# Prompt attention with value products in runs and 1024-column exponentials, reserved buffers, held first loads, and a last MLP step without Strassen's sums

## The chip, the cores and the metric

The kernel runs on one core of one Trainium2 chip. The core has TensorE for matmuls (PE in the profile, its weight loads PEld), VectorE (DVE), ScalarE (ACT), GpSimd (POOL) and SyncE (SP, which here only issues DMAs), an on-chip memory of 128 partitions (SBUF), and the matmul accumulators (PSUM, eight banks of 512 fp32 columns). The metric is device time in microseconds (us) of one execution, from the inputs in device memory to all outputs written. A lower time is better.

## What is computed

One inference step of a one-layer decoder: 2048 prompt tokens, and 8 sequences of 8 new tokens each with 8192 cached positions. Everything is fp32. Model width is 1024, the MLP's hidden width 4096.

- One input projection gives the queries, keys, values and forget gates of 8 attention heads of width 64 ("FoX"), and queries, keys, values and gates of 4 mLSTM heads of width 128.
- FoX attention of the prompt is causal softmax with a forgetting bias:

```python
s = jnp.einsum('bqhd,bkhd->bhqk', q_i, k).astype(jnp.float32) * scale
s = s + L_i[..., :, None] - L[:, :, None, :]
s = jnp.where(k_pos[None, :] <= q_pos[:, None], s, -jnp.inf)
p = jax.nn.softmax(s, axis=-1)
return jnp.einsum('bhqk,bkhd->bqhd', p.astype(v.dtype), v)
```

- The new tokens attend over their paged caches; the mLSTM heads run a chunked recurrence with a matrix state; the mLSTM output is normalised and multiplied by an output gate.
- Both are joined, go through the output projection, a residual layer norm, and the MLP:

```python
mix = jnp.concatenate([fox_h, mn.astype(x.dtype)], axis=-1) @ w_o
x1 = _layer_norm(DN_ALPHA * x + mix, ln1_g, ln1_b)
hid = jnp.square(jax.nn.relu(x1 @ w1))
return _layer_norm(DN_ALPHA * x1 + hid @ w2, ln2_g, ln2_b)
```

Outputs are the tokens, and keys, values, gates and states of prompt and samples.

## The kernel before

**Matmuls.** Large products are made of three fast matmuls: each operand is split into a rounded high part (`split_hi`, ACT, L154) and the rest (`split_lo`, DVE, L157); `mm3` (L162) multiplies high by high, high by low and low by high. Transposes and the value products of attention use plain fp32 matmuls.

**Order.** The program is written in Python and unrolled. A planner assigns each engine's instructions an order by a simulated time line; program order is the priority, so an instruction may be placed ahead of earlier ones when its operands and its buffer are ready in that simulation. On the chip each engine and each DMA queue keeps the planned order. `tc.issue_after(ins)` puts an instruction behind another of the same engine; `add_manual_dep` with class `Sync` makes it wait for another engine's instruction. Tiles come from pools; a tile name with `bufs=n` is a ring of n buffers. Pools of a later phase lie on the memory of pools that were closed, tiles in the order in which their names are first asked for, and the first write of a tile waits for the old tiles that lay there.

**Stages.**
1. Input projection (`block_a`, to about 888 us): four blocks of 512 prompt tokens. The mLSTM recurrence (`m_block`) and cached attention run between its pieces, a step at a time (`tick`, `beside`). Each mLSTM chunk ends in `norm_out` (L614): statistics on DVE, a power on POOL, four normalising instructions on DVE, the output gate's multiply on POOL (L627), then four transposes on PE (L632). In the last block's last value pass `begin_b` (L220) loads the first keys and queries of attention.
2. Prompt attention (`phase_b`, about 888 to 1338 us): 64 units, 8 heads × 8 groups of 256 queries. `scores` (L957) makes for each of two query tiles the products with the keys in pieces of up to 512 columns (L975, L976), adds the bias while taking the maximum on DVE (L982, L986) and puts the result into a score tile `S`. `values` (L993) takes the exponentials on ACT with their row sums (L1003), turns the probabilities on PE four 128×128 tiles at a time into a PSUM tile `pt` (L1016, three buffers), copies them to `PT` (ACT L1019 or DVE L1021), and multiplies by the values (L1025). Within a unit the products of four key tiles follow those four tiles' transposes. The scores of unit n+1 stand in the program ahead of the values of unit n. `head` takes the tiles of a head (values `vn`, bias `nl`, keys `ks`), in rings of two. POOL adds up parts of the second MLP weight in memory meanwhile (`w2_sum`).
3. Output projection and first layer norm (`phase_o`, to about 1562 us).
4. MLP (`phase_c`): four blocks of 512 prompt tokens; the last also holds the 64 sample rows. Each has 8 steps p. `hidden(p, half)` makes 256 hidden columns of either half; `output(p)` adds their product with `w2` to the result rows `y`. Output uses Strassen's scheme: a 2 × 2 split (token halves × hidden halves), seven products of sums instead of eight, sums of `w2` made ahead in memory, sums of hidden values on DVE (`made`, L1392), and each product added to one or more result parts (`add`, L1362). When a row's last contribution is in, `add` takes its statistics (L1370), and `norm_quick` (L187) normalises it and stores it.

Of the kernel before, what the change touches and what calls it, by code (L numbers as in the profile page):

```python
# [10 lines left out]
F32 = mybir.dt.float32  # L11
F32R = mybir.dt.float32r
# [13 lines left out]
S = 2048  # L26
# [26 lines left out]
def body(ctx, tc, I, O, stages):  # L53
# [166 lines left out]
    def begin_b():  # L220

        bf["kn"] = pf.tile([128, 512], F32, name="kn0")
        bf["qn"] = pf.tile([128, 256], F32, name="qn0")
        for d in range(2):
            SY.dma_start(bf["kn"][d * 64:d * 64 + 64], O["k_prompt"][0:64, 0:512])
        for d in range(2):
            SY.dma_start(bf["qn"][d * 64:d * 64 + 64], dq[0, 0:64, 0:256])

# [384 lines left out]

    def norm_out(hh, np_, og, tok0):  # L614

# [10 lines left out]
        hf = hh.rearrange("p h e -> p (h e)")  # L626
        G.tensor_tensor(hf, hf, og, op=OP.mult)  # L627

# [40 lines left out]
    def m_block(bi):  # L669
# [10 lines left out]
        for c in range(bi * 4, bi * 4 + 4):  # L680
# [41 lines left out]
            for p in range(2):  # L722
                yield 1
                pc = ppm.tile([128, 2, 129], F32, name="mn", tag="mm", bufs=2)
                for i in range(2):
                    T.matmul(pc[:, i], kw[:, 2 * p + i], va_[:, 2 * p + i], start=True, stop=True)
# [168 lines left out]
    def phase_b():  # L895
# [15 lines left out]
        def head(h):  # L911
            vn = Z[0]["vn"] if h == 0 else pb.tile([128, 16, 64], F32, name="vn", bufs=2)
            nl = pb.tile([128, 2048], F32, name="nl", bufs=2)
            if h == 0:
                masks.append(pb.tile([128, 128], F32, name="dmask"))
            ls = pb.tile([128, 32], F32, name="ls", bufs=2)
            ks = pb.tile([128, 2048], F32R, name="ks", bufs=2)
            G.memset(ls, 1.0)
            return dict(h=h, ls=ls, nl=nl, vn=vn, ks=ks)
# [7 lines left out]
        def keys_load(h, g):  # L927
            kn = pb.tile([128, 512], F32, name="kn", bufs=3)
            for d in range(2):
                SY.dma_start(kn[d * 64:d * 64 + 64], kp[h * 64:h * 64 + 64, g * 512:(g + 1) * 512])  # L930
            return kn
# [11 lines left out]
        def queries(z, g):  # L943

            h = z["h"]
            qn = bf["qn"] if h == g == 0 else pb.tile([128, 256], F32, name="qn", bufs=3)
# [3 lines left out]
            if h == 0 and g == 0:  # L950
                z["vn"] = pb.tile([128, 16, 64], F32, name="vn", bufs=2)
            ql = pb.tile([128, 256], F32R, name="ql", bufs=3)
            split_hi(qh, qn)
            split_lo(ql, qn, qh)
            z["q", g] = qh, ql

        def scores(z, g):  # L957
# [4 lines left out]
            for i in range(2):  # L962
# [8 lines left out]
                for a in range(0, n, 512):  # L971
# [21 lines left out]
        def values(z, g, sc):  # L993
# [3 lines left out]
            for i, (st, mx) in enumerate(sc):  # L997
                qt = 2 * g + i
                n = (qt + 1) * 128
                lp = pb.tile([128, 4], F32, name="lp", bufs=6)  # L1000
                for k, sp in enumerate(st):
                    w = min(512, n - k * 512)
                    last["ACT"] = A.activation(sp[:, :w], sp[:, :w], AF.Exp, bias=mx[:, 7:8], accum_out=lp[:, k:k + 1])  # L1003
                V.tensor_reduce(z["ls"][:, qt:qt + 1], lp[:, :len(st)], axis=AX.X, op=OP.add)

            po = ppb.tile([128, 256], F32, name="po", bufs=1)
            nk = 2 * g + 2
            for k0 in range(0, nk, 4):
                PT = pb.tile([128, 4, 256], F32, name="PT", bufs=4)
                for i in range(2):  # L1010
                    kk = min(4, 2 * g + i + 1 - k0)
# [3 lines left out]
                    for k in range(kk):  # L1015
                        T.transpose(pt[:, k], sc[i][0][k0 // 4][:, k * 128:(k + 1) * 128], ident)  # L1016
                    dst = PT[:, :kk, i * 128:i * 128 + 128]
                    if i == 0 or (k0 // 4) % 2 != 0:
                        A.copy(dst, pt[:, :kk])  # L1019
                    else:  # L1020
                        V.tensor_copy(dst, pt[:, :kk])  # L1021
                for k in range(k0, min(k0 + 4, nk)):
                    q0 = 128 if k == nk - 1 else 0
                    c = (k % 2) * 64
                    last["PE"] = T.matmul(po[c:c + 64, q0:], z["vn"][:, k], PT[:, k - k0, q0:],  # L1025
                                          start=(k < 2), stop=(k >= nk - 2), skip_group_check=True)
                tick(0.45 * min(4, nk - k0))
            if g % 4 == 0:
# [24 lines left out]

        masks = []
# [6 lines left out]
        dmask = masks[0]  # L1061
        pad(pb, 64)
# [6 lines left out]
        for n in range(len(units) + LA):  # L1069
            if 10 <= n < 16 and acc[1] is not None:  # L1070
                attend()
            w2_due[0] += 64 * (n % 8 // 2 + 1) / 130 if n >= 8 else 0
            while n and len(w2_done) < min(64, w2_due[0]):
                w2_sum()
# [201 lines left out]
    def phase_c():  # L1276
# [51 lines left out]
        for ci, blk in enumerate(CB):  # L1328
# [28 lines left out]
            def add(t, half, ps, op=OP.add):  # L1357
# [16 lines left out]
            def operands(p):  # L1374
# [39 lines left out]
            def output(p, ahead, begun=None):  # L1414
# [13 lines left out]
                for at_, n in enumerate(order):  # L1428
                    kind, first_, last_, r0, half, op = plan[n]
                    if p == 7 and at_ == 2 and ci == 3:  # L1430
                        C["gb"] = vecs(2)
                    for m in order[:at_ + 3]:
# [28 lines left out]
                if begun:  # L1461
                    for hf in range(2):
                        turn(ci + 1, 4, hf, begun)

            def y_out(t):
                return O["y_sample"].rearrange("b t d -> (b t) d") if t == 16 else O["y_prompt"][0, t * 128:(t + 1) * 128]
# [478 lines left out]
```

## Time and profile before

| | |
|---|---|
| Median of 3 runs | 3236.75 us (3231.51 to 3241.11) |
| Profiled execution | 3245.35 us |
| Its span, first to last instruction | 3242.4 us |
| PE, DVE, ACT, POOL busy | 96%, 65%, 46%, 28% |
| Mean granted TensorE clock | 0.987 |
| DMA | 734.34 MB, mean 226 GB/s |

Rows of the profile are read so: a line number (L1025) is that of the kernel; `out<-in` are tile names; `xN` counts instructions; in time lines the first number is the start in us, the second the duration, and a bracket at the end holds the idle time before it and what ended it. Busy time of PE includes the filling and draining of its pipeline, so neighbouring matmuls overlap in the list. Rows of line 154, 157, 163, 164, 165 belong to helpers and are told apart by their tiles.

### The profile page before, as it was taken

The numbers are of one execution on the slowest core, as the hardware profiler recorded it, in microseconds if no ns is written. First come the engines' busy times: TensorE is split into PE (matmuls) and PEld (weight loads), VectorE is DVE, ScalarE is ACT, GpSimd is POOL, SyncE is SP. The second block draws the span as 40 slices with busy tenths as digits, with TensorE's granted clock in tenths as the row PEclk, the third lists the DMA queues.
The fourth block names the chain that finished last, engine by engine and source line by source line (L and its number), as shares of the span: only waits on it lengthen the run. The fifth ranks groups of instructions, "written<-read, shape, count | busy, mean of one in ns | idle before, by whom it ended". The sixth has DMA issues, their size and how long they took to land. (4 is left out here: it accounts for less than half of the span.)

```text
span 3242.4 us, 57713 instructions
## 1 busy us (share of the span) xinstructions
PE 3127.7 (96%) x21585; PEld 2535.8 (78%) x21585; DVE 2095.6 (65%) x5062; ACT 1489.0 (46%) x2940; POOL 907.2 (28%) x974
## 2 busy tenths in 40 slices
PE   8899999999989999999999999999999999899997
PEld 8898998998956666677677777776777777698895
DVE  6866657456478788544466568656586665766658
ACT  3342343343378888522344345343454444344442
POOL 0021233323334333276233423433333121000000
PEclk9999999999989999999999999999999999999999
DMA  5465776866667776487887878868779766543322
GB/s 188 128 220 174 254 225 202 277 238 232 228 220 204 185 181 150 171 300 262 294 291 277 296 270 308 317 243 328 289 282 338 279 212 210 208 147 137 121 95 81
DMA packets 339775, 734.34 MB, mean 226 GB/s; under 512 B 63656, under 2 KB 177704, under 8 KB 338600
## 3 DMA queue, kind: packets, MB, share of 16 engines
q1 hardware_dynamic: 252360, 416.18, 39.2%
q0 software_dynamic: 83520, 304.12, 26.7%
q10 hardware_dynamic: 3616, 10.36, 0.9%
q8 instruction: 170, 2.79, 0.3%
q14 instruction: 109, 0.89, 0.1%
HBM read 677.71 MB, written 86.38 MB: 236 GB/s over the span
## 5 line engine op out<-in xcount | busy, mean ns | idle before, releaser
L157 DVE TENSOR_TENSOR wl<-wr,wh 128x1024 fp32r<-128x1024 f32 x300 | 366.0, 1222 | 249.5 <-ACT wh L154 241.9
L163 PE MATMUL ph<-x1h,wh 128*128 128x512 f32 (+1 forms) x1280 | 455.2, 356 | 0.0
L164 PE MATMUL ph<-x1l,wh 128*128 128x512 f32 (+1 forms) x1280 | 453.0, 354 | 0.2 <-DVE x1l L157 0.2
L165 PE MATMUL ph<-x1h,wl 128*128 128x512 f32 (+1 forms) x1280 | 450.5, 354 | 0.7 <-DVE wl L157 0.4
L154 ACT ACTIVATE wh<-wr 128x1024 fp32r<-128x1024 f32 x300 | 315.4, 1053 | 290.1 <-PE ph L164 162.4
L1662 POOL DMA_INDIRECT kT<-cache_k,idxK x256 | 275.8, 1077 | 540.7 <-PE sQ L1685 477.2
L163 PE MATMUL py<-wh,hh 128*128 128x512 f32 x896 | 358.3, 403 | 6.4 <-ACT hh L154 3.7
L164 PE MATMUL py<-wl,hh 128*128 128x512 f32 x896 | 352.4, 395 | 5.5 <-DVE wl L157 5.5
L165 PE MATMUL py<-wh,hl 128*128 128x512 f32 x896 | 349.2, 395 | 2.1 <-DVE hl L157 2.1
L1362 DVE TENSOR_TENSOR y<-y,py 128x512 f32<-128x512 f32 x416 | 281.5, 682 | 98.9 <-PE py L165 94.8
L163 PE MATMUL pm<-xh,whi 128*128 128x256 f32 (+1 forms) x1024 | 299.5, 292 | 0.0
L164 PE MATMUL pm<-xl,whi 128*128 128x256 f32 (+1 forms) x1024 | 295.5, 289 | 0.0
L165 PE MATMUL pm<-xh,wlo 128*128 128x256 f32 (+1 forms) x1024 | 294.5, 288 | 0.0
L1773 POOL DMA_INDIRECT vt<-cache_v,idxV x164 | 177.7, 1084 | 384.3 <-PE sO L1797 316.9
L163 PEld LDWEIGHTS ph<-x1h,wh 128*128 128x128 f32 x1280 | 241.2, 188 | 40.8 <-issue 7.8
L165 PEld LDWEIGHTS ph<-x1h,wl 128*128 128x128 f32 x1280 | 240.3, 188 | 37.1 <-issue 3.7
L164 PEld LDWEIGHTS ph<-x1l,wh 128*128 128x128 f32 x1280 | 241.2, 188 | 34.4 <-issue 3.3
L163 PE MATMUL pm<-whi,xh 128*128 128x256 f32 (+2 forms) x816 | 238.1, 292 | 9.4 <-ACT whi L154 8.4
L164 PE MATMUL pm<-wlo,xh 128*128 128x256 f32 (+2 forms) x816 | 233.8, 287 | 0.6 <-DVE wlo L157 0.6
L165 PE MATMUL pm<-whi,xl 128*128 128x256 f32 (+2 forms) x816 | 233.4, 286 | 0.0
L163 PEld LDWEIGHTS py<-wh,hh 128*128 128x128 f32 x896 | 169.0, 189 | 60.4 <-issue 14.5
L1003 ACT ACTIVATE S<-S,mx 128x512 f32<-128x512 f32 (+2 forms) x320 | 207.7, 652 | 18.4 <-DVE mx L989 17.1
(363 smaller groups left out, 6829.1 us busy)
## 6 DMA issues: line engine op xcount, KB each, us to landing
wr<-w SPq DMA_DIRECT2D x200, 512.0 KB
wra<-w_in SPq DMA_DIRECT2D x104, 512.0 KB
wr<-dw SPq DMA_DIRECT2D x96, 512.0 KB
dw<-w POOLq DMA_DIRECT2D x48, 512.0 KB, 8.1
Rb<-dR SPq DMA_DIRECT2D x128, 128.0 KB
kT<-dw SPq DMA_DIRECT2D x32, 512.0 KB
kT<-w SPq DMA_DIRECT2D x24, 512.0 KB
xn<-xp_t SPq DMA_DIRECT2D x16, 512.0 KB
```

The costliest lines, as they stand in the source:

```text
L154: last["ACT"] = A.activation(dst, src, AF.Copy, scale=scale)
L157: r = (eng or V).tensor_tensor(dst, src, hi.bitcast(F32), op=OP.subtract)
L163: T.matmul(ps, wh, xh, start=first, stop=False, skip_group_check=shared)
L164: T.matmul(ps, wh, xl, start=False, stop=False, skip_group_check=shared)
L165: last["PE"] = T.matmul(ps, wl, xh, start=False, stop=stop, skip_group_check=shared)
L1003: last["ACT"] = A.activation(sp[:, :w], sp[:, :w], AF.Exp, bias=mx[:, 7:8], accum_out=lp[:, k:k + 1])
L1362: V.tensor_tensor(y, y, ps, op=op)
L1662: G.indirect_dma_start(out=piece(n), out_offset=None, in_=ck, in_offset=IO(ap=idxK[:, b, j // 2, j % 2:j % 2 + 1], axis=0))
L1773: vx["last"] = G.indirect_dma_start(out=vt.rearrange("p f c -> p (f c)"), out_offset=None, in_=cv, in_offset=IO(ap=idxV[:, b, (kt % 4) * 4 ...
```

## The change

- `begin_b`: the four first loads of keys and queries wait for the PE instruction that was the last one recorded when they are asked for, and stand in the order keys, queries, keys, queries.
- `norm_out` takes an engine: for the last chunk (15) the gate's multiply runs on DVE instead of POOL.
- `phase_b`: the first key buffer of the ring, then `vn0`, `nl0`, `ks0`, and the first query buffer are asked for before other tiles; heads use `vn`, `nl`, `ks` by parity under two names instead of rings of two; `dmask` comes later.
- Score tiles are 1024 columns wide, seven of them instead of ten of 512; an exponential covers up to 1024 columns.
- In `values` all transposes of a unit come first, and each value product is put behind the last of them; the `tick` there goes (it triggered nothing in this stage).
- MLP: four buffers instead of three for split hidden values; two operands instead of one made ahead in the last step of a block; in the last block's last step `plain` takes the place of `output`: eight products without sums, one result tile after another. Two of its four weight tiles are loaded and split inside the last `hidden` (`early`), and the layer norm's vectors are asked for at its head. The count at which `add` takes statistics follows from that.

```diff
@@ begin_b
+        at = last["PE"].ins.name
         for d in range(2):
-            SY.dma_start(bf["kn"][d * 64:d * 64 + 64], O["k_prompt"][0:64, 0:512])
-        for d in range(2):
-            SY.dma_start(bf["qn"][d * 64:d * 64 + 64], dq[0, 0:64, 0:256])
+            for t, x in (("kn", O["k_prompt"][0:64, 0:512]), ("qn", dq[0, 0:64, 0:256])):
+                r = SY.dma_start(bf[t][d * 64:d * 64 + 64], x)
+                tc.add_manual_dep(r.ins, at,
+                                  mybir.DependencyInfo(mybir.DependencyClass.Sync, mybir.DependencyReason.DATA), reason="late")
@@ norm_out
-        G.tensor_tensor(hf, hf, og, op=OP.mult)
+        (eng or G).tensor_tensor(hf, hf, og, op=OP.mult)
...
-                    norm_out(hh, 128, og, t0)
+                    norm_out(hh, 128, og, t0, V if c == 15 else None)
@@ phase_b
-            vn = Z[0]["vn"] if h == 0 else pb.tile([128, 16, 64], F32, name="vn", bufs=2)
-            nl = pb.tile([128, 2048], F32, name="nl", bufs=2)
+            e = h % 2
+            vn, nl, ks = homes.pop(h, None) or (pb.tile([128, 16, 64], F32, name=f"vn{e}"),
+                                                pb.tile([128, 2048], F32, name=f"nl{e}"),
+                                                pb.tile([128, 2048], F32R, name=f"ks{e}"))
...
-            kn = pb.tile([128, 512], F32, name="kn", bufs=3)
+            kn = kns.pop() if kns else pb.tile([128, 512], F32, name="kn", bufs=3)
...
-                    sp = pb.tile([128, 512], F32, name="S", bufs=10)
-                    st.append(sp)
+                    if a % 1024 == 0:
+                        st.append(pb.tile([128, 1024], F32, name="S", bufs=7))
+                    sp = st[-1][:, a % 1024:a % 1024 + 512]
...
-                    w = min(512, n - k * 512)
+                    w = min(1024, n - k * 1024)
...
+                        turned = T.transpose(pt[:, k], sc[i][0][k0 // 8][:, c:c + 128], ident)
...
-                for k in range(k0, min(k0 + 4, nk)):
...
+            for k in range(nk):
+                q0 = 128 if k == nk - 1 else 0
+                c = (k % 2) * 64
+                with tc.issue_after(turned.ins):
+                    last["PE"] = T.matmul(po[c:c + 64, q0:], z["vn"][:, k], PTs[k // 4][:, k % 4, q0:],
                                           start=(k < 2), stop=(k >= nk - 2), skip_group_check=True)
-                tick(0.45 * min(4, nk - k0))
...
+        kns = [pb.tile([128, 512], F32, name="kn", bufs=3)]
+        homes = {}
+        homes[0] = (pb.tile([128, 16, 64], F32, name="vn0"), pb.tile([128, 2048], F32, name="nl0"),
+                    pb.tile([128, 2048], F32R, name="ks0"))
...
+        qns = [pb.tile([128, 256], F32, name="qn", bufs=3)]
@@ phase_c
-                if ci == 3 and due[t, half] == 8 * sums[blk.index(t) // 2, half]:
+                if ci == 3 and due[t, half] == 7 * sums[blk.index(t) // 2, half] + (2 if t == 16 else 1):
...
-                    h = ph.tile([128, 2, 256], F32R, name="hh", bufs=3)
+                    h = ph.tile([128, 2, 256], F32R, name="hh", bufs=4)
...
+            def weight(src):
+                wr = spare().rearrange("p (k c) -> p k c", k=2)
+                SY.dma_start(wr, src.rearrange("p (k c) -> p k c", k=2))
+                return (*piece(None, wr), wr)
...
+            def plain(p):
+                f = H.pop((p, 0)), H.pop((p, 1))
+                C["gb"] = vecs(2)
...
+                for n in range(2):
+                    part(0, n)
+                for q in (1, 3):
+                    lastw[q] = weight(I["w2"][p, q])
+                for n in range(2):
+                    part(1, n)
+                for half in range(2):
+                    ps = ppc.tile([128, 512], F32, name="ph", tag="ph", bufs=2)
+                    for k in range(2):
+                        two_sides(ps, [(f[n][:, k, 512:576], lastw[n * 2 + half][2][:, k]) for n in range(2)], k == 0, k == 1)
+                    for n in range(2):
+                        add(16, half, ps[n * 64:n * 64 + 64])
+                for i in range(4):
+                    r, c = i // 2, slice(i % 2 * 128, i % 2 * 128 + 128)
+                    for half in range(2):
+                        ps = ppc.tile([128, 512], F32, name="py", bufs=4)
+                        for n in range(2):
+                            (h, l), (wh, wl, _) = x[r, n], lastw[n * 2 + half]
+                            for k in range(2):
+                                mm3(ps, h[:, k, c], l[:, k, c], wh[:, k], wl[:, k], n == k == 0, n == k == 1, True)
+                        add(blk[i], half, ps)
+
+            def early():
+                for q in (0, 2):
+                    lastw[q] = weight(I["w2"][7, q])
...
+                if p == 7 and ci == 3:
+                    plain(p)
+                    break
...
-                    pre.append(ahead(p, 1))
+                    pre.append(ahead(p, *order[:2]))
...
-                    hidden(p + 1, 1, sampled if p == 6 and ci == 2 else None)
+                    hidden(p + 1, 1, {2: sampled, 3: early}.get(ci) if p == 6 else None)
```

`part(r, n)` inside `plain` splits one quarter of the hidden values into its high and low part.

More of the change, by code (lines that the diff above doesn't have):

```diff
@@ L945, in queries @@
             h = z["h"]
-            qn = bf["qn"] if h == g == 0 else pb.tile([128, 256], F32, name="qn", bufs=3)
+            qn = bf["qn"] if h == g == 0 else qns.pop() if qns else pb.tile([128, 256], F32, name="qn", bufs=3)
             for d in range(2 if h or g else 0):
@@ L999, in values @@
                 n = (qt + 1) * 128
-                lp = pb.tile([128, 4], F32, name="lp", bufs=6)
+                lp = pb.tile([128, 2], F32, name="lp", bufs=6)
                 for k, sp in enumerate(st):
-                    w = min(512, n - k * 512)
+                    w = min(1024, n - k * 1024)
                     last["ACT"] = A.activation(sp[:, :w], sp[:, :w], AF.Exp, bias=mx[:, 7:8], accum_out=lp[:, k:k + 1])
@@ L1015, in values @@
                     for k in range(kk):
-                        T.transpose(pt[:, k], sc[i][0][k0 // 4][:, k * 128:(k + 1) * 128], ident)
+                        c = k0 % 8 * 128 + k * 128
+                        turned = T.transpose(pt[:, k], sc[i][0][k0 // 8][:, c:c + 128], ident)
                     dst = PT[:, :kk, i * 128:i * 128 + 128]
@@ L1058, in phase_b @@
         queries(Z[0], 0)
+        qns = [pb.tile([128, 256], F32, name="qn", bufs=3)]
         Z[0].update(head(0))
         last.pop("POOL", None)
-        dmask = masks[0]
+        dmask = pb.tile([128, 128], F32, name="dmask")
         pad(pb, 64)
@@ L1072, in phase_b @@
             w2_due[0] += 64 * (n % 8 // 2 + 1) / 130 if n >= 8 else 0
-            while n and len(w2_done) < min(64, w2_due[0]):
+            while n and len(w2_done) < min(60 if False else 64, w2_due[0]):
                 w2_sum()
```

27 lines of the change are left out of this document (15 added, 12 removed).

## The prediction

> **What bounds the kernel now.** I read the table of stages first (busy time of each engine in stretches of the span, then granted TensorE clock, DMA share, GB/s), because the change touches four places and leaves the rest alone.
>
> ```profile
> 888.00:940.00 52.00, 39.38 (x206) 26.66 (x204) 37.84 (x144) 31.88 (x88) 13.87 (x24) 0.80 0.60 170
> 940.00:1338.00 398.00, 390.28 (x2689) 271.17 (x2687) 314.72 (x1244) 333.38 (x938) 139.18 (x218) 1.00 0.66 175
> 1338.00:1350.00 12.00, 8.02 (x30) 6.06 (x28) 9.13 (x9) 7.00 (x8) 6.02 (x4) 0.86 0.66 219
> 1350.00:3196.00 1846.00, 1806.27 (x11130) 1404.62 (x11129) 1160.13 (x2025) 780.10 (x1201) 509.68 (x469) 0.99 0.69 249
> 3196.00:3242.40 46.40, 24.16 (x101) 16.08 (x99) 42.37 (x73) 7.67 (x11) 5.41 (x5) 0.87 0.18 63
> ```
>
> The columns are PE, PEld, DVE, ACT, POOL. Prompt attention runs from about 888 to 1338. In its body (second row) PE is busy 98% of the time at full clock, so only less PE time or fewer PE gaps pay there; ACT is at 84%, DVE at 79%. Its first 52 us are another matter: 206 matmul records, where the body's rate (2689 in 398 us, 6.76 per us) would need 30.5 us. Some 21 us are lost at the start. The hand-over to the output projection (third row) has 30 matmuls in 12 us. The last 46 us belong to DVE: 42.37 busy against 24.16 of PE. Between 1350 and 3196, where PE is 98% busy, the change touches almost nothing. The cut at 3196 is where the matmuls of the last hidden unit end.
>
> **1. The start of attention (reserved homes, held loads, the multiply on DVE).** Four views of the same 15 us: PE, POOL, SP queue and ACT in order of time, then a row of the stage table.
>
> ```profile
> 887.75 1.05 PE L726 MATMUL mn<-va,kw 128*128 128x129 f32 x8
> 891.58 0.93 PE L632 MATMUL mm<-ident,hh 128*128 128x128 f32 x4 [2.78 <-POOL hh L627]
> 892.76 0.58 PE L975 MATMUL pS<-ks,qh 128*128 128x256 f32 x1 [0.24 <-DVE ks L157]
> ...
> 900.92 1.11 PE L975 MATMUL pS<-ks,qh 128*128 128x384 f32 x2 [1.23 <-ACT qh L154]
> ```
>
> ```profile
> 890.26 1.26 POOL L627 TENSOR_TENSOR hh<-hh,og 128x512 f32<-128x512 f32 x1 [1.88 <-DVE hh L625]
> ```
>
> ```profile
> 892.45 1.29 SPq L930 DMA_DIRECT2D kn<-k_prompt  x2
> ```
>
> ```profile
> 900.45 0.42 ACT L154 ACTIVATE qh<-qn 128x256 fp32r<-128x256 f32 x1 [3.00 <-DMA qn<-dq]
> ```
>
> ```profile
> 892.00:905.50 13.50, 8.57 (x27) 5.38 (x25) 7.21 (x29) 4.72 (x14) 3.63 (x7) 0.50 0.76 203
> ```
>
> PE first waits 2.78 us for POOL's multiply of 1.26 us; on DVE the same shape costs about 0.67 (the add of part 4's rows) with no change of engine, so about 0.6 to 0.8 us goes. What is late next is the key split (892.76 waited for it). The larger loss follows: the second group's keys are asked for only at 892.45 and its queries reach ACT at 900.45, so PE starts its second round of scores at 900.92, and all of 892 to 905.5 runs at clock 0.50. In the code the tiles that the new kernel reserves first (kn, vn0, nl0, ks0: 6 + 4 + 8 + 8 KB) fall on the early addresses of the projection's pool, which held conv constants, token tiles and raw weights, dead well before 888; before, the key tiles came after the score tiles and lay on operands of the projection's last matmuls. So those loads can be issued ahead of the state outputs instead of behind them, and the first key split need not wait for the last matmul.
>
> The fill of small units stays a chain (scores, max, exponential, transpose, product), so I take 8 of the 21 us. Bounds: −15, if most of it goes, and +3, if a reserved tile lands on something late, one more wait like the 2.78 us. The Trainium skill (TensorE: Matmul & The Clock Gate, Part 1) says that an idle window of about 3.4 us halves the clock and a sustained busy one restores it; here gaps of 2.78 us and less kept it at 0.50 for 13.5 us. By that rule the slow stretch would shrink to about one window, an estimate of 3 us more gain; the sum leaves it out.
>
> The hold itself costs nothing unless it is late. These loads stood far ahead:
>
> ```profile
> L225 SPq DMA_DIRECT2D kn<-k_prompt x2: 531/560/588, 183.7 to 184.3; - x2
> ```
>
> Now four DMAs wait on SP for the last matmul issued before the last value pass begins, and what stands behind them on SP are stores of v_prompt and loads of attention tiles. Their use is the first score at 892.76, more than a whole pass of 96 matmuls later. Taken at 0, bounds −1 to +2.
>
> **2. Value products in runs.** PE in order of time in the body; x is the number of records merged.
>
> ```profile
> 1194.88 1.08 PE L1025 MATMUL po<-PT,vn 128*64 128x256 f32 x8
> 1195.89 0.50 PE L975 MATMUL pS<-ks,qh 128*128 128x512 f32 x1
> ...
> 1197.91 1.51 PE L1025 MATMUL po<-PT,vn 128*64 128x256 f32 x12
> 1199.36 0.66 PE L1016 MATMUL pt<-ident,S 128*128 128x128 f32 x4
> ...
> 1202.83 1.94 PE L1025 MATMUL po<-PT,vn 128*64 128x256 f32 x16
> 1204.70 0.50 PE L975 MATMUL pS<-ks,qh 128*128 128x512 f32 x1
> ```
>
> From the start of a run to the start of what follows: 8 records 1.01 us, 12 records 1.45, 16 records 1.87. That is 0.1075 a record plus 0.15 fixed: each run costs 0.15 us more than its products. Groups by line and shape in the attention stage give the totals:
>
> ```profile
> L1025 PEld LDWEIGHTS po<-PT,vn 128*64 128x64 f32 x1152 | 72.8, 137 | 54.3 <-issue 12.7 <-DVE ot L1033 3.5 <-DVE mx L982 3.1
> ...
> L1003 ACT ACTIVATE S<-S,mx 128x512 f32<-128x512 f32 x224 | 160.0, 717 | 15.9 <-DVE mx L989 14.6 <-DVE ls L1004 1.0
> ...
> L1003 ACT ACTIVATE S<-S,mx 128x128 f32<-128x128 f32 x32 | 12.6, 394 | 1.5 <-DVE mx L989 1.5
> ```
>
> 1152 records in runs of about 10 (an estimate from this stretch) are 115 runs. With all products behind the unit's last transpose the least is one per unit, 64. 51 runs × 0.15 = 7.7 us. Score matmuls of the next unit can still cut in, but entering a run may cost too, so I take −7, bounds 0 to −13.
>
> **3. Exponentials of 1024 columns.** Per head, tiles of up to 512 columns need 40 exponentials and tiles of 1024 need 24: over 8 heads 320 become 192. From the two rows, 384 columns cost 323 ns, so 1024 columns take about 717 + 431 = 1148 ns instead of 1434, and one accumulator read fewer: some 0.3 us × 128 = 38 us of ACT. ACT is not the bound. What reaches PE is its wait for exponentials:
>
> ```profile
> PEld pt L1016 <- ACT S L1003: 12.6, 17, 3.2
> ```
>
> Most of that is in the start. Against the gain stands a first transpose that waits for 1024 columns instead of 512, 0.43 us later. The score ring grows from ten tiles of 512 to seven of 1024 (20 to 28 KB), which lets two large units (8 tiles) nearly fit. I take −2, bounds +10 (0.43 us exposed in each of the 24 or so largest units) to −5.
>
> **Leaving attention.** PE, then ACT, around the end of the stage.
>
> ```profile
> 1336.33 1.94 PE L1025 MATMUL po<-PT,vn 128*64 128x256 f32 x16
> 1340.64 0.51 PE L163 MATMUL pw<-wh,mh 128*128 128x512 f32 x1 [2.38 <-ACT wh L154]
> 1342.75 0.80 PE L164 MATMUL pw<-wl,mh 128*128 128x512 f32 x1 [1.60 <-DVE wl L157]
> ```
>
> ```profile
> 1339.55 3.88 ACT L154 ACTIVATE wh<-wr 128x1024 fp32r<-128x1024 f32 x4
> ```
>
> The four weight splits start only after attention's last product, since their buffers lie on the value tiles of the last head. In the new order that memory belongs to even heads and key loads, free eight units earlier, so the splits can lie beside attention. 2.38 + 1.60 us of waits go, the input tile's own split (it lies on score tiles) stays: −4, bounds 0 to −6.
>
> **4. The last MLP step.** Groups by line and shape after 3196, and the last rows of PE and of DVE.
>
> ```profile
> L1362 DVE TENSOR_TENSOR y<-y,py 128x512 f32<-128x512 f32 x14 | 9.2, 670 | 0.0
> L157 DVE TENSOR_TENSOR wl<-kT,wh 128x1024 fp32r<-128x1024 f32 x5 | 6.1, 1218 | 0.7 <-ACT wh L154 0.7
> ```
>
> ```profile
> 3224.72 0.39 PE L164 MATMUL py<-wl,hh 128*128 128x512 f32 x1
> 3224.95 0.39 PE L165 MATMUL py<-wh,hl 128*128 128x512 f32 x1
> ```
>
> ```profile
> 3236.14 2.73 DVE L197 SCALAR_TENSOR_TENSOR y<-y,ln_r,b 128x512 f32<-128x512 f32 x4
> ```
>
> PE: 7 products × 12 matmuls (84) become 8 × 12 (96); at 0.23 us a matmul that is +2.8 us. The sample rows' 16 records stay. DVE, per instruction some 0.06 less than its mean, since neighbours overlap (four L197 in 2.73): seven adds go (14 + 5 become 8 + 4), −4.3; four operand sums go, −2.5; of five weight splits in the stretch two remain, 3 × 1.14 = −3.4; of five activation splits three remain, −1.2 (a Strassen step has seven of each, of which two are made before 3196). Statistics and normalisation stay. So DVE falls from 42.4 to about 31 us, and from 3196 would end at about 3228. PE from 3196 needs 96 × 0.23 + 3.6 for the sample rows = 25.7, so to 3222; then the last tile's add, statistics, POOL's power and four normalising steps, about 5 us: 3227. The two limits agree: DVE ends at 3228 instead of 3238.87. −10, bounds −13 to +3 (PE's added time alone, if DVE's relief is not on the path). The tiles now finish one by one, where before they all closed at the end.
>
> **Small edits.** Four buffers instead of three for the split activations remove at most the wait in this row of the page; −1. Making two operands ahead in the earlier blocks only reorders the same instructions; 0.
>
> ```profile
> L163 PE MATMUL py<-wh,hh 128*128 128x512 f32 x896 | 358.3, 403 | 6.4 <-ACT hh L154 3.7
> ```
>
> **Sum.** −8 − 7 − 2 − 4 − 10 − 1 = −32 us. The profiled execution took 3245.35 us (span 3242.4), so it would take 3213; it lies 8.6 us above the median of the runs, 3236.75. From the median: 3205 us, 1.0% faster.
>
> **Rivals.**
> - *Only the last step pays.* The stages after attention keep their own pace, and attention's start stays a chain. Then −10: 3227. For it: DMA is 0.6 to 0.66 busy in attention, and the second group's queries were late by DMA. Against: after 1350 PE is busy for 1806 of 1846 us, so time gained before it is not waited away.
> - *Slower: runs starve on evacuation.* A large unit now turns up to eight tiles of four transposes with three PSUM banks, while ACT must first finish exponentials of 1.15 us in order. If each of the 32 larger units (groups 4 to 7 of eight heads) waits for two of them, 2.3 us, that is +74, and with the rest −32: 3279. It decides from 1.0 us a unit. The body's PE gaps are now only 398 − 390.28 = 7.7 us and ACT gains 38 us of room, which speaks against it. The skill's page on TensorE (A second HAM failure mode) says that PE pausing between groups while PSUM banks cycle can make the clock oscillate; no row of this body shows it (clock 1.00).
> - *No change.* The tail's gain is spent by the 0.43 us latency of part 3 and a late held load: 3237.
>
> **How the numbers follow.** Forecast of part sums 0.60, only the last step 0.20, no change 0.10, slower 0.10. A measurement of this kernel can tell about 0.3%, 10 us, so "only the last step" sits at that edge and counts as faster at 0.15 and as unchanged at 0.05: faster 0.75, same 0.14, slower 0.11. The range for 8 in 10 runs from 3184 (the gains of parts 1, 2 and 4 at their ends, partly) to 3234, which takes in the tail-only case.
>
> **What would show it.** Right: the second round of scores starts near 893 to 895, not 900.9; product runs mostly of 16 to 32 records in large units; 192 exponentials; first projection matmul within 2 us of the last product; DVE's last instruction about 32 us after the last hidden matmul, not 43. Wrong: PE waits on exponentials or on PT copies that grow above 20 us in the body, a clock below 1.00 after 940, or a hold that moves the first score past 893.

## The result, and the profile after

The changed kernel takes 3214.24 us (median of 6 runs, 3210.17 to 3216.76) where the kernel before took 3238.24 beside it: a ratio of 0.9921, 95% interval 0.9906 to 0.9936. Two later comparisons gave 0.9911 and 0.9917. So the gain is about 25 us, a little under the 32 that the prediction summed up, and most of it doesn't come from where the prediction put it.

The table of stages of the changed kernel (start and end, length, then busy time of PE, PEld, DVE, ACT, POOL, granted clock, DMA share, GB/s), cut within 1 us of the same events as the prediction's rows: the projection, the start and the body of attention, the hand-over, the tail.

```profile
0.00:875.76 875.76, 854.06 (x7445) 805.92 (x7446) 531.46 (x1569) 327.67 (x697) 231.66 (x258) 1.00 0.67 219
875.76:928.00 52.24, 42.31 (x237) 28.01 (x236) 43.81 (x169) 34.26 (x82) 13.33 (x24) 0.87 0.65 191
928.00:1316.00 388.00, 378.57 (x2654) 270.67 (x2652) 310.16 (x1219) 294.72 (x689) 138.50 (x217) 0.99 0.68 176
1316.00:1328.00 12.00, 8.17 (x22) 6.29 (x23) 9.14 (x9) 6.89 (x8) 5.02 (x3) 0.72 0.75 273
3175.30:3213.80 38.50, 26.79 (x112) 19.00 (x112) 30.71 (x55) 2.31 (x4) 5.14 (x5) 0.91 0.17 62
```

The same stages of the kernel before, for the lengths that the prediction's rows don't hold:

```profile
887.75:1338.30 450.55, 430.18 (x2894) 298.08 (x2892) 352.56 (x1387) 365.31 (x1025) 153.60 (x242) 0.97 0.66 174
1338.30:1350.60 12.30, 8.35 (x29) 6.58 (x30) 9.13 (x9) 7.00 (x8) 5.72 (x4) 0.86 0.69 235
3195.90:3242.40 46.50, 24.25 (x102) 16.18 (x100) 42.47 (x73) 7.70 (x11) 5.41 (x5) 0.87 0.18 62
```

Three things moved. The projection's last matmul starts at 875.1 instead of 887.6, though the change puts nothing ahead of it but a wait. From there to the start of attention's last value product it is 440.4 us instead of 450.3. The tail is 38.50 instead of 46.50, with DVE busy for 30.71 instead of 42.47. The hand-over to the output projection did not move: its first matmul starts 2.8 us after that last product in both.

One profile is not enough to split 25 us: the same program differs from itself. The changed kernel's attention, measured so from start to start, lasted 440.4, 446.9 and 442.2 us in three profiled executions, and the MLP, with its reads of the cache, 1629 to 1641 over all fourteen profiles, whatever was changed. So the experiments below give a ratio of times, and beside it the length of the stage concerned in all profiles.

### The profile page after: what moved, and what is told of

It is laid out like the page before. It is cut to its first block, busy times and chain, and to the rows that moved or that the text cites. A ratio compares the mean times of both kernels' runs of the same rounds, so it can differ in the third digit from the quotient of the medians.

```text
span 3213.8 us, 57419 instructions
## 1 busy us (share of the span) xinstructions
PE 3124.1 (97%) x21597; PEld 2538.6 (79%) x21597; DVE 2082.2 (65%) x5046; ACT 1446.8 (45%) x2678; POOL 910.1 (28%) x973
## 5 line engine op out<-in xcount | busy, mean ns | idle before, releaser
L163 PE MATMUL py<-wh,hh 128*128 128x512 f32 x900 | 358.8, 403 | 10.4 <-DVE y L1369 6.4
L157 DVE TENSOR_TENSOR wlo<-wra,whi 128x1024 fp32r<-128x1024 f32 (+1 forms) x112 | 141.6, 1266 | 102.0 <-ACT whi L154 95.5
```

The costliest lines, as they stand in the source:

```text
L157: r = (eng or V).tensor_tensor(dst, src, hi.bitcast(F32), op=OP.subtract)
L163: T.matmul(ps, wh, xh, start=first, stop=False, skip_group_check=shared)
```

## The experiments

Each edit is on the kernel before unless it says otherwise. Ratios are to the kernel before, run on the same chip.

### The hold alone

```diff
@@ begin_b
+        at = last["PE"].ins.name
         for d in range(2):
...
+                r = SY.dma_start(bf[t][d * 64:d * 64 + 64], x)
+                tc.add_manual_dep(r.ins, at,
```

> The kernel before, with the hold of the first loads alone. Theory A (head of the line): in the kernel before, SP stood 5.7 us in the first block (141.9 to 147.66) in front of the held query load, which waits for the store of the queries, and weight loads stood behind it; with the hold the projection ends 8 to 9 us earlier (its last matmul near 879 instead of 887.75), the rest keeps its lengths, total 3229, ratio 0.997. Theory B (the prediction): the loads were early anyway and their place costs nothing; the projection ends within 2 us of 887.75, total 3238, ratio 1.000.

Ratio 0.9971 (0.9955 to 0.9988): some 9 us (4 to 15) from an edit that only makes four loads later. Theory A holds. SP's DMA issues in order of time in the kernel before, around the place:

```profile
140.99 0.84 SPq L585 DMA_DIRECT2D dq<-st  x2
147.66 1.13 SPq L227 DMA_DIRECT2D qn<-dq  x2
148.88 0.54 SPq L587 DMA_DIRECT2D dqb<-qr  x1
149.51 0.40 SPq L585 DMA_DIRECT2D dq<-st  x1
150.01 0.39 SPq L654 DMA_DIRECT2D Wm<-dM  x1
```

and with the hold:

```profile
139.94 0.80 SPq L587 DMA_DIRECT2D dq<-st  x2
141.52 0.32 SPq L589 DMA_DIRECT2D dqb<-qr  x1
141.98 0.39 SPq L587 DMA_DIRECT2D dq<-st  x1
142.47 0.37 SPq L656 DMA_DIRECT2D Wm<-dM  x1
```

The first query load `qn` had been planned into the first block, right behind the store of the queries that it reads. It has to wait until that store has landed, and SP issues nothing meanwhile. The waits of SP in that stretch (engine, line, what it waited for: us, times, longest) have it as `SPq L227`. Behind it stood the load of `Wm`, the mLSTM's mask matrix, 7.5 us later than with the hold. POOL masks `Wm` at 157.47 instead of 150.16, multiplies `hh` by the output gate at 163.00 instead of 155.72, and PE waits for that multiply. The two share no data: this `Wm` belongs to the next chunk. DVE had the input of POOL's power (`r`) ready at 151.05, but POOL took it only at 160.43, behind the mask. So the late load also held up POOL's queue. DVE's and POOL's rows before:

```profile
150.88 0.17 DVE L622 TENSOR_SCALAR r<-mv 128x4 f32<-128x4 f32 x1
```

```profile
157.47 0.64 POOL L687 TENSOR_SCALAR_AFFINE_SELECT Wm<-Wm 128x512 f32<-128x512 f32 x1 [52.93 <-ACT Wm L686]
...
160.43 1.05 POOL L623 TENSOR_TENSOR r<-r,nhalf 128x4 f32<-128x4 f32 x1
```

SP's and PE's waits before:

```profile
SPq L227 <- DMA dq<-st: 5.7, 1, 5.7
PE mm L632 <- POOL hh L627: 6.5, 1, 6.5
```

PE's wait with the hold, and then 40 us of stages, before and with the hold (PE 31.85 busy against 39.12):

```profile
PE mm L634 <- POOL hh L629: 0.3, 1, 0.3
```

```profile
130.00:170.00 40.00, 31.85 (x233) 31.57 (x234) 31.55 (x116) 12.33 (x29) 5.34 (x6) 0.91 0.56 162
```

```profile
130.00:170.00 40.00, 39.12 (x303) 38.83 (x304) 36.49 (x136) 14.34 (x33) 5.88 (x7) 1.00 0.67 193
```

Over all profiles, projection matmuls 1000 to 1040 take 13.7 to 15.6 us in the six kernels without the hold of the queries, 7.8 in this one, and 7.6 to 8.2 in the other seven with it. The projection ends at 878.5 to 887.6 (mean 882.3) in those six, and at 871.7 to 882.1 (mean 876.1) in the eight profiles with it: 6.2 us, the rest of the 12 is difference between executions.

### Which of the held loads

```diff
-            SY.dma_start(bf["kn"][d * 64:d * 64 + 64], O["k_prompt"][0:64, 0:512])
+            r = SY.dma_start(bf["kn"][d * 64:d * 64 + 64], O["k_prompt"][0:64, 0:512])
+            tc.add_manual_dep(r.ins, last["PE"].ins.name,
...
         for d in range(2):
             SY.dma_start(bf["qn"][d * 64:d * 64 + 64], dq[0, 0:64, 0:256])
```

> The kernel before, with the hold on the two key loads alone; the two query loads stay where they were. Theory A (head of the line): the wait that matters is that of the query load for the queries' store; it stands in SP's queue as before, the load of the first block's mask matrix behind it stays late, PE waits 5 to 6.5 us for the state's output there, the projection matmuls 1000 to 1040 take 13.7 to 15.6 us as in every kernel without the hold (7.8 to 8.2 with both held), and the time stays, ratio 0.999 to 1.001. Theory B: it is the early traffic or the place of these loads as such, and half of them held gives about half: some 11 us for those matmuls, ratio 0.9985.

Ratio 1.0013 (1.0000 to 1.0026), and matmuls 1000 to 1040 take 13.7 us. SP and PE still stand at the same place:

```profile
SPq L229 <- DMA dq<-st: 4.2, 1, 4.2
PE mm L634 <- POOL hh L629: 4.6, 1, 4.6
```

So it is the query load at the head of SP's queue. The key loads, which before the change were issued at 183.7 after a wait of 1.6 us for a store of their own, gave nothing when held. Theory B falls. The query loads were not held by themselves; that they are the ones follows by difference.

### The last MLP step alone

```diff
+                if p == 7 and ci == 3:
+                    plain(p)
+                    break
...
-                    h = ph.tile([128, 2, 256], F32R, name="hh", bufs=3)
+                    h = ph.tile([128, 2, 256], F32R, name="hh", bufs=4)
```

> The kernel before, with the plain last MLP step alone (its four buffers and early weights included). The prediction's term: the stretch after the last hidden matmul falls from 46.5 to about 36 us, total 3228, ratio 0.997. Measured in the full change: 46.5 to 38.5, which gives 3230. Rival: the plain step's added 12 matmuls and its weights in front of the last hidden half cost 3 to 4 us before the last hidden matmul (the MLP stage grew from 1633.6 to 1637.9 in the full change), so that only 4 us are left, total 3234, ratio 0.999.

Ratio 0.9957 (0.9933 to 0.9982). The tail is 38.6 us in this profile:

```profile
3197.80:3236.40 38.60, 26.93 (x113) 19.09 (x112) 30.84 (x55) 2.43 (x4) 5.15 (x5) 0.91 0.17 62
```

This is the steadiest number of the study: 46.4 to 46.9 us in the six profiles without the plain step, 38.7 to 38.8 in the eight with it (from the last hidden matmul's start). The rival falls too: the last three eighths of the hidden matmuls, in which two weight tiles are now loaded and split early, take 353.7 us against 354.1 before. The MLP's growth that the rival rested on (1633.6 to 1637.9) lies ahead of that, in the part with the cache reads, and kernels without the edit have it too (1639.7 with the runs alone). By the ratio the edit is worth some 14 us (6 to 22); the tail shows 8 of them, and the rest is not placed.

### Runs of products alone, wide exponentials alone

The first edit keeps scores of 512 columns, and holds the products back behind the unit's last transpose:

```diff
+            for k in range(nk):
+                with tc.issue_after(turned.ins):
+                    last["PE"] = T.matmul(po[c:c + 64, q0:], z["vn"][:, k], PTs[k // 4][:, k % 4, q0:],
```

> The kernel before, with the value products of a unit behind its last transpose alone; exponentials stay at 512 columns. Theory A (the prediction): each run of products costs 0.15 us to enter and leave, 116 runs become about 98, so 2.7 us, and with the other order of the transposes up to 8; first scores to last product falls from 445.1 to 437 to 442, total 3231 to 3235. Theory B: the gain of the stage (445.1 to 435.0 in the full change) comes from the wider exponentials and the wider score buffers, and this edit alone gives 0 or costs (transposes wait for three PSUM banks while the products are held back): 445 to 450, total 3238 to 3243.

The second has the wide score tiles, and the products where they were:

```diff
-                    sp = pb.tile([128, 512], F32, name="S", bufs=10)
+                    if a % 1024 == 0:
+                        st.append(pb.tile([128, 1024], F32, name="S", bufs=7))
```

> The kernel before, with score buffers and exponentials of 1024 columns alone. Theory A (the prediction): ACT gains 38 us and is not the bound, so first scores to last product falls by 2 us, 445.1 to 443, total 3236. Theory B: the wider score buffers let the planner run further ahead and PE lose less to waits, so that most of the 10 us are here: 435 to 438, total 3228 to 3231.

The runs alone cost: ratio 1.0023 (1.0006 to 1.0039), some 7 us. The wide exponentials alone gain: 0.9980 (0.9968 to 0.9992), some 6 us. The prediction had them the other way round. The largest waits of PE's transposes (into `pt`) from the first scores to the end of attention (us, times, longest): before, with the runs, with the wide exponentials, and with the full change.

```profile
PE pt L1016 <- ACT S L1003: 7.0, 6, 2.8
```

```profile
PE pt L1018 <- ACT PT L1021: 4.9, 4, 2.5
PE pt L1018 <- DVE PT L1023: 3.5, 11, 0.5
PE pt L1018 <- ACT S L1003: 3.2, 3, 1.5
```

```profile
PE pt L1018 <- ACT PT L1021: 4.0, 1, 4.0
PE pt L1018 <- ACT S L1004: 3.1, 2, 1.9
```

```profile
PE pt L1019 <- ACT PT L1022: 5.8, 3, 3.0
```

With the runs, transposes wait for a PSUM tile `pt` to be copied out, 8.4 us in 15 waits (rows of ACT and DVE), where the kernel before has 0.4 us and the other four with narrow exponentials and no runs have 0.4 to 4.2. That is the mechanism of the prediction's rival on evacuation, at a ninth of its price (8.4 us against 74). And there are fewer runs to gain from than counted: 116 before, 101 with this edit, 98 in the full change, not 64, since the planner lets score matmuls and transposes in between. With wide exponentials, the waits for exponentials are 3.1 us instead of 7.0. That doesn't show where the gain comes from: 5.6 of the 7.0 lie in the first 52 us, the other four kernels with narrow exponentials and no runs have 3.2 to 7.2, and a wait of 4.0 for a copy of `pt` stands beside them.

The lengths of attention say the same: 446.3 to 450.3 us in the five profiles with narrow exponentials and no runs (mean 447.8), 452.5 with runs, 441.0 with wide exponentials.

### The changed kernel without its runs, and with the second queries early

Three kernels and the changed kernel as yardstick, on one chip. First the yardstick:

> The changed kernel once more, as the yardstick on this chip for the three variants beside it: 0.9906 to 0.9936 of the kernel before, the projection ending near 875, first scores to last product 435.

0.9911 (0.9882 to 0.9941); its projection ended at 882.1 and its attention took 446.9 us, the one far from the first profile.

Without runs:

```diff
-            for k in range(nk):
...
-                with tc.issue_after(turned.ins):
...
+                for k in range(k0, min(k0 + 4, nk)):
```

> The changed kernel with the value products back behind each group of four transposes (everything else kept). Theory A: the runs cost time by themselves (+2.3 parts in a thousand alone, 7 us), so without them 4 to 7 us are won, 3208 to 3210, ratio 0.990, and first scores to last product falls from 435 to about 430. Theory B: beside 1024-column exponentials the runs neither cost nor gain (the wide exponentials alone gave 435.8, the full change 435.0), 3214, ratio 0.992, 434 to 437. Theory C (the prediction): the runs gain, so without them 3 to 7 us are lost, 3218 to 3221.

0.9926 (0.9902 to 0.9951) beside 0.9911, with medians of 3215.06 and 3215.01: no difference that can be measured, as Theory B says, but the intervals take in some 10 us either way, so Theory C's 3 to 7 us are not excluded. The lengths agree with B: 443.2 us is the mean of three profiles of the changed kernel, and 443.2 the mean of the two with wide exponentials and no runs and late queries. The stage table of attention shows that the runs do save what the prediction counted, and lose it again. First the two without runs (wide exponentials alone, and this kernel), then two of the changed kernel:

```profile
881.20:1322.30 441.10, 425.77 (x2893) 295.84 (x2891) 349.67 (x1387) 330.84 (x769) 154.85 (x242) 0.98 0.68 178
876.10:1321.60 445.50, 426.00 (x2893) 295.71 (x2891) 352.06 (x1388) 330.29 (x769) 153.02 (x241) 0.98 0.66 176
```

```profile
875.76:1316.00 440.24, 420.88 (x2889) 298.68 (x2887) 353.97 (x1388) 328.98 (x770) 151.83 (x240) 0.98 0.68 178
882.30:1329.30 447.00, 422.91 (x2893) 299.74 (x2891) 355.43 (x1388) 329.70 (x769) 152.46 (x241) 0.97 0.67 175
```

PE is busy for 425.8 and 426.0 us without runs, and for 420.9 and 422.9 with them. Its idle time (length less busy time) is 15.3 and 19.5 without, 19.4 and 24.1 with them. Some 20 runs fewer (120 to 98) thus take about 4 us off PE's busy time, where 0.15 us a run would give 3, and the idle time grows by as much. With narrow exponentials the one profile shows no such saving: 428.1 us busy with the runs, 427.8 to 430.2 in three without. Why the runs cost alone and not here is left open; that ACT, relieved of 36 us, copies `pt` sooner would explain it, but no run shows it.

Second queries early:

```diff
+        bf["q1"] = pf.tile([128, 256], F32, name="qn1")
-            for t, x in (("kn", O["k_prompt"][0:64, 0:512]), ("qn", dq[0, 0:64, 0:256])):
+            for t, x in (("kn", O["k_prompt"][0:64, 0:512]), ("qn", dq[0, 0:64, 0:256]), ("q1", dq[0, 0:64, 256:512])):
```

> The changed kernel with the queries of the second unit loaded with the held first loads too, instead of last in SP's queue at the start of attention. In the full change the second round of scores begins at 887.85, 12.1 us after the last state matmul, behind the split of queries whose load was issued at 882.16. Theory A: that load is all the second round waits for; it then begins 4 to 5 us earlier, some 7 us after the last state matmul, total 3210, ratio 0.9908. Theory B: the next wait takes its place (the exponentials, the value tile, the second keys) and the first product comes no earlier: 3214, ratio 0.992.

0.9912 (0.9885 to 0.9939), no difference to the yardstick. The second round does come early, 1.1 us after the first instead of 7.4, but by the 37th score matmul the lead is gone (28.2 us after the first score, 26.3 in the changed kernel). DVE's, ACT's and PE's rows of this profile show where it went:

```profile
902.16 0.15 DVE L990 TENSOR_REDUCE mx<-mx 128x1 f32<-128x3 f32 x1
```

```profile
903.96 0.42 ACT L154 ACTIVATE qh<-qn 128x256 fp32r<-128x256 f32 x1 [1.50 <-DMA qn<-dq]
904.28 1.13 ACT L1004 ACTIVATE S<-S,mx 128x1024 f32<-128x1024 f32 x1
```

```profile
905.56 0.66 PE L1020 MATMUL pt<-ident,S 128*128 128x128 f32 x4 [3.55 <-ACT S L1004]
```

An exponential stands in ACT's queue behind the split of queries that haven't landed, and PE waits 3.55 us. The exponential's maximum was ready at 902.31 and ACT idle from 902.46 to 903.96, so some 1.8 us of these are due to the place in the queue, by an estimate from these rows. It is the same pattern as on SP: a wait at the head of a queue delays what is ready behind it. The Trainium skill (TensorE: Matmul & The Clock Gate, Part 1, its paragraph on engine queue depths) calls ACT and DVE strict first-in first-out; this row agrees.

Both:

> The two edits together: products behind each group of four transposes and the second unit's queries loaded early. If each is worth what it is alone, the sum: with theory A of both 3204, ratio 0.989; with theory B of both 3214, ratio 0.992.

0.9913 (0.9887 to 0.9940). Nothing to add up.

Timed longer, the changed kernel and the early queries:

> The changed kernel, as the yardstick for the variant beside it on the same chip: a ratio of 0.9915 to 0.992 to the kernel before.

> The changed kernel with the second unit's queries loaded early, timed longer. In the look before, the second round came 6.4 us earlier but the 36th score matmul came no earlier than without the edit, behind waits for exponentials that stand in ScalarE's queue behind splits of the next query loads. Theory A: gained early is kept, 4 us, ratio 0.990 where the changed kernel beside it has 0.9915. Theory B: given back within 25 us, the same ratio as the changed kernel beside it to 0.001.

0.9917 (0.9898 to 0.9936) and 0.9912 (0.9892 to 0.9933), medians 3211.50 and 3212.14. Theory B: given back. No version here beats the changed kernel by more than can be measured.

### The order of the buffers and the multiply on DVE, alone

```diff
+        kns = [pb.tile([128, 512], F32, name="kn", bufs=3)]
+        homes = {}
+        homes[0] = (pb.tile([128, 16, 64], F32, name="vn0"), pb.tile([128, 2048], F32, name="nl0"),
+                    pb.tile([128, 2048], F32R, name="ks0"))
...
-                    norm_out(hh, 128, og, t0)
+                    norm_out(hh, 128, og, t0, V if c == 15 else None)
```

> The kernel before, with the buffers in the other order and the last chunk's multiply on VectorE, alone. The prediction's terms for it: the second round of scores 6 to 8 us earlier (13.2 us after the last state matmul becomes 5 to 7) and 4 us at the end of attention (first projection matmul 2 us or less after the last product instead of 2.8, its two waits of 2.38 and 1.60 gone): total 3226, ratio 0.9963. Theory now: the second round waits for its query load, which stays last in SP's queue, so only the multiply's 1 us comes, and the end of attention stays as it was: 3237, ratio 0.9997.

Ratio 1.0005 (0.9993 to 1.0017). The start and the end of attention on PE:

```profile
884.29 0.74 PE L632 MATMUL mm<-ident,hh 128*128 128x128 f32 x4 [2.50 <-DVE pad_4x L85]
885.99 0.58 PE L972 MATMUL pS<-ks,qh 128*128 128x256 f32 x1 [0.95 <-DVE ks L157]
...
892.29 1.11 PE L972 MATMUL pS<-ks,qh 128*128 128x384 f32 x2 [0.56 <-ACT qh L154]
...
1329.90 0.50 PE L163 MATMUL pw<-wh,mh 128*128 128x512 f32 x1 [2.38 <-ACT wh L154]
1332.02 0.80 PE L164 MATMUL pw<-wl,mh 128*128 128x512 f32 x1 [1.62 <-DVE wl L157]
```

The wait for POOL (2.78 us) has become one of 2.50 for DVE: the multiply is shorter (0.63 us against 1.26), but on DVE it starts only at 883.61, behind a state update of 0.60 us and two memsets, where POOL could start as soon as the four normalising instructions were done. The second round of scores starts 6.3 us after the first instead of 8.2, still behind the query load. The two waits at the end are those of before to 0.02 us. So the order of the buffers and the multiply, which the prediction gave 12 us, give nothing that can be measured.

### What adds up

In parts of a thousand: hold −2.9, last step −4.3, wide exponentials −2.0, runs +2.3, buffers +0.5; together −6.4, against −7.9, −8.9 and −8.3 measured for the whole. The difference of some 6 us lies within the intervals of five ratios; the missing part would fit runs that no longer cost beside wide exponentials. The sum is no closer check than that: of the 4.3 parts of the last step, the tail itself shows 2.4.

## Why the prediction came out right, and where it was wrong

The forecast of 3205 us, 1.0% faster, had the sign and nearly the size (0.8%). Term by term:

- **The hold: 0 forecast, about −6 to −9 measured.** The step that failed is "the hold itself costs nothing unless it is late", with the row of the key load as its proof. The key load indeed stood far ahead, and holding it gained nothing. The query load beside it isn't in the prediction: its row in SP's waits says 5.7 us. The prediction asked what the hold adds in front of SP's later work, and not what it takes away from the place where the loads had stood.
- **The start of attention: −8 forecast, about −0.5 measured in the full change, −1.6 with this edit alone.** The step that failed is the memory argument, that reserved tiles let the second group's loads go ahead of the state outputs. One of the two key loads moved up past one of those stores; the query loads kept their place last. The second round of scores moved from 12.4 to 11.9 us after the last state matmul in the full change, and to 10.8 with this edit alone. (The 13.2 and 12.1 in the expectations are counted from different ones of its eight matmuls.) And the early-queries run shows that a repair of that wait is given back within 25 us, so that even the right move was not worth 8.
- **Runs of products: −7 forecast, between 0 and +7.** Beside wide exponentials the price of a run came near: PE's busy time fell by about 4 us for some 20 runs fewer. The count failed (98 runs, not 64), and the cost of holding products back was left in a rival: waits, for `pt` among others, that cost as much as was saved.
- **Exponentials: −2 forecast, −6.5 measured (2.6 to 10.4).** The duration was right: 1148 ns forecast, 1153 measured. "ACT is not the bound" is true of the sum (84% busy before), yet relieving it gained more than forecast. The term was too small; which waits of PE gave the rest stays open, as said above.

```profile
L1003 ACT ACTIVATE S<-S,mx 128x1024 f32<-128x1024 f32 x80 | 92.1, 1153 | 40.7 <-DVE mx L989 39.8 <-DVE ls L1004 0.6
```

  The Trainium skill (ScalarE: Activation LUTs, What ACT_TABLE_LOAD costs) gives about 280 ns plus 0.833 ns a column, by an estimate 1133 ns here; the row agrees to 2%.
- **Leaving attention: −4 forecast, 0 measured.** Same failed step, that other memory lets work start earlier: ACT takes the copy of the last output, the input tile's split and the four weight splits in the same order as before, and the first projection matmul comes 2.8 us after the last product in all fourteen profiles. Why the planner kept that order isn't shown.
- **The last step: −10 forecast, −8 measured.** The mechanism was right: DVE's busy time fell to 30.71 us ("about 31"), and PE's last product came 26.8 us after the last hidden matmul (25.7 forecast). What was missed is that DVE no longer works without a pause. It waits for PE early in the tail, where before the same adds waited 0.1 in all, and these 4 us are taken off its gain of 11.8. DVE's last instruction ends 35.0 us after the last hidden matmul, where 32 were forecast. DVE's groups by line in the tail of the changed kernel (busy, mean ns, idle before them):

```profile
L1369 DVE TENSOR_TENSOR y<-y,py 128x512 f32<-128x512 f32 x8 | 5.4, 678 | 2.0 <-PE py L165 1.9
...
L1369 DVE TENSOR_TENSOR y<-y,ph 64x512 f32<-64x512 f32 x4 | 2.7, 684 | 2.1 <-PE ph L170 2.0
```

- **Small edits: −1 forecast;** not measured apart from the last step, with which the fourth buffer was tried. PE's waits for `hh` in the MLP, which that buffer was to remove, are 2.1 us before and 3.2 with the full change.
- **A sign of being wrong that did appear.** The prediction named a clock below 1.00 after 940. The body of the changed kernel has 0.99: two stretches of 3.4 us at 0.50, each around the end of a wait for ACT's copy of `pt` (PE's rows, then the stage table for the first). The kernel before has one such stretch in its body, at 1130.75. So the rival on evacuation, laid aside for a body at clock 1.00, did take a small part.

```profile
1049.42 0.78 PE L1019 MATMUL pt<-ident,S 128*128 128x128 f32 x4 [2.57 <-ACT PT L1022]
...
1107.94 1.33 PE L1019 MATMUL pt<-ident,S 128*128 128x128 f32 x5 [3.04 <-ACT PT L1022]
```

```profile
1049.80:1053.20 3.40, 3.40 (x16) 2.76 (x16) 2.39 (x11) 3.01 (x9) 0.00 (x0) 0.50 1.02 201
```

So two terms of 12 us fell out, a term of 0 was worth 6 to 9, and two terms of attention missed in opposite directions. The total was right by luck, because errors cancelled; only the last step was right for its reason.

## What to carry to other kernels

Before a load is called free because it is early, look up what it waits for on its queue, and what stands behind it: an early load that waits for a store holds up the whole queue, and here holding it back gained some 9 us without touching any arithmetic. When one wait is repaired, name the engine whose queue holds the next one; at the start of this pipeline the lead was spent by the units that followed. A stage whose bounding engine was 98% busy still gained 0.2% from relief of a second engine. And a saving in one engine's busy time is not yet a gain: the runs of products took 4 us off PE's and gave it back in waits.

## What the runs showed that was not expected

- The landing of one store, seen by the load that waits for it at the head of SP's queue, took 4.2 to 5.7 us in the six profiles without the hold of the queries, and PE's loss followed it: 4.6 to 4.9 us behind 4.2, 5.2 behind 4.4, 5.9 behind 5.4, 6.5 behind 5.7.
- The slow clock at the start of attention outlasts most of PE's gaps there. In the changed kernel, and then with the second queries early, where the second round of scores has no wait:

```profile
879.30:892.80 13.50, 8.64 (x26) 5.53 (x26) 7.94 (x34) 4.98 (x15) 3.21 (x7) 0.50 0.75 215
```

```profile
876.40:886.50 10.10, 8.48 (x29) 4.96 (x27) 6.73 (x30) 5.36 (x15) 3.31 (x7) 0.50 0.74 189
```

With the gaps mostly closed the stretch shortens from 13.5 to 10.1 us: PE was busy for 8.48 of 10.10 us and the granted clock stayed at 0.50. The prediction's side estimate, that closing the gaps would give 3 us more by a faster clock, did not come true: the stretch lost 3.4 us, but after the wait of 3.55 us shown above the same profile is at 0.50 for 3.4 us again (907.0 to 910.4).
